# The first load of a batched matmul as one transfer of 128 partitions, or as one of 16 and one of 112

## The chip, the cores and the metric

The kernel runs on one core of a Trainium2 chip. The metric is the device time of one execution in microseconds (us), given as the median of several runs. A profile of one execution stands beside it; its span, from the first to the last instruction that it shows, is about 2 us shorter than the time. Inside the core, TensorE (PE) multiplies, VectorE (DVE) and ScalarE (ACT) copy and cast, GpSimd (POOL) prepares an identity matrix, and SyncE (SP) issues most transfers. All transfers of the core run on the same 16 DMA engines.

## The reference

Sixteen products of 512 x 512 matrices in float32; both operands come transposed.

```python
def setup_inputs():
    batch, m, k, n = 16, 512, 512, 512
    return {
        "a": np.random.randn(batch, k, m).astype(np.float32),
        "b": np.random.randn(batch, n, k).astype(np.float32),
    }

def reference(a, b):
    return np.matmul(a.transpose(0, 2, 1), b.transpose(0, 2, 1)).astype(np.float32)
```

The inputs are 16.8 MB each and the output is 16.8 MB: 50.33 MB pass between HBM and SBUF, each byte once.

## The kernel before

Each engine has a program of its own, and they are tied by semaphores. SyncE loads a and b. The batch is taken in 16 items i; two items make a pair q (or p, for b). A load of a is either one item (1 MB, 128 partitions with a row of 8 KB each) or, for the pairs in WIDE, a whole pair (2 MB). A load of b is always a pair (2 MB). There are three buffers for each.

```python
    a_v = a.rearrange("b (ki ko) m -> b ki ko m", ko=KO)      # one item: 128 partitions x 8 KB
    a_w = a.rearrange("(p g) (ki r) m -> p (g ki) r m", g=2, r=2 * KO)
    WIDE = range(1, 6)
    LOADS = 3                                                 # buffers of a; PAIRS = 3 of b
    # ...
        def load_a(sp, i):
            q, g = divmod(i, 2)
            s, use = q % LOADS, q // LOADS
            if use:
                sp.wait_ge(summed, MO * (2 * (q - LOADS) + 1) + 1)
            if q in WIDE:
                sp.dma_start(a_sb[s][:], a_w[q]).then_inc(a_in[2 * s], 16)
            else:
                sp.dma_start(a_sb[s][:, g * KO:(g + 1) * KO], a_v[i]).then_inc(a_in[2 * s + g], 16)

        def loaded_a(q, g):                # semaphore and value that the cast of (q, g) waits for
            g = 0 if q in WIDE else g
            uses = [u for u in range(q + 1) if u % LOADS == q % LOADS and (g == 0 or u not in WIDE)]
            return a_in[2 * (q % LOADS) + g], 16 * len(uses)
```

SyncE issues the first item of a, then the first two pairs of b with the second item of a between or after them, and goes on in that manner; from the fourth pair on it waits for buffers to come free. At the end it issues the last stores.

```python
        def run_sp(sp):
            for i in range(B):
                if i == 0:
                    load_a(sp, 0)
                for p in ([0] if i == 0 else [(i + 1) // 2] if i % 2 and i + 1 < B else []):
                    if p >= PAIRS:
                        sp.wait_ge(turned, p - PAIRS + 1)
                    sp.dma_start(b_sb[p % PAIRS][:], b_v[p]).then_inc(b_in[p % PAIRS], 16)
                # ... wait for an earlier store
                if i and not (i % 2 and i // 2 in WIDE):
                    load_a(sp, i)
            # ... the stores of the last pairs; the last one waits for its copies:
            sp.wait_ge(last_go, 3)
            store(sp, H - 1, slice(1, 2))
```

ScalarE waits for a load of a and casts it to bfloat16; VectorE waits for a load of b and casts it. TensorE transposes b (128 x 128 at a time, against the identity), VectorE copies the result to SBUF, and TensorE multiplies. VectorE and ScalarE copy the sums out of PSUM, and the stores are issued by ScalarE and, for the last pairs, by SyncE.

```python
        def cast_a(act, i):
            q, g = divmod(i, 2)
            sem_, value = loaded_a(q, g)
            act.wait_ge(sem_, value)
            # ... act.copy(a_bf[i % 2] <- a_sb[q % LOADS])
```

Of the kernel before, what the change touches and what calls it, by code (L numbers as in the profile page):

```python
# [11 lines left out]
def kernel(  # L12
# [7 lines left out]
    P = 128  # L20
    B, K, M = a.shape
    _, N, _ = b.shape
    KO = K // P
# [12 lines left out]
    a_v = a.rearrange("b (ki ko) m -> b ki ko m", ko=KO)  # L36
# [4 lines left out]
    WIDE = range(1, 6)  # L41
    LOADS = 3
# [11 lines left out]
    with tc.tile_critical(sync_engine=nc.gpsimd.engine):  # L54
# [3 lines left out]
        a_sb = [sb(f"a_sb{s}", [P, 2 * KO, M], f32) for s in range(LOADS)]  # L58
# [12 lines left out]
        a_in = [sem(f"a_in{s}") for s in range(2 * LOADS)]  # L71
# [22 lines left out]
# [4 lines that stand above are left out]
            if use:  # L98

                sp.wait_ge(summed, MO * (2 * (q - LOADS) + 1) + 1)  # L100
            if q in WIDE:
                sp.dma_start(a_sb[s][:], a_w[q]).then_inc(a_in[2 * s], 16)
            else:
                sp.dma_start(a_sb[s][:, g * KO:(g + 1) * KO], a_v[i]).then_inc(a_in[2 * s + g], 16)

        def loaded_a(q, g):

            g = 0 if q in WIDE else g
            uses = [u for u in range(q + 1) if u % LOADS == q % LOADS and (g == 0 or u not in WIDE)]
            return a_in[2 * (q % LOADS) + g], 16 * len(uses)  # L110

        def run_sp(sp):
            for i in range(B):
# [8 lines that stand above are left out]
                if i % 2 == 0 and i // 2 >= OUTS:  # L122

                    sp.wait_ge(o_out[i // 2 % OUTS], 16 * (i // 2 // OUTS))
                if i and not (i % 2 and i // 2 in WIDE):
                    load_a(sp, i)

            for j in range(H - TAIL, H - 1):
                sp.wait_ge(summed, MO * (2 * j + 2) + 3)
                store(sp, j)  # L130

            sp.wait_ge(summed, MO * (B - 1) + 1)
            sp.wait_ge(half_go, 1)
            store(sp, H - 1, slice(0, 1))
            sp.wait_ge(last_go, 3)
            store(sp, H - 1, slice(1, 2))
# [17 lines left out]
# [5 lines that stand above are left out]
            x, to = a_sb[q % LOADS], a_bf[i % 2]  # L159
            act.wait_ge(sem_, value)  # L160
            if q in WIDE:
                own = slice(g * P // 2, (g + 1) * P // 2)
                for s in range(2):
                    copy = act.copy(to[s * P // 2:(s + 1) * P // 2], x[own, s * KO:(s + 1) * KO, :])  # L164
            else:
                copy = act.copy(to[:], x[:, g * KO:(g + 1) * KO, :])  # L166
            copy.then_inc(ac_go, 1)
# [150 lines left out]
```

## Time and profile before

| | |
|---|---|
| time, median of 3 runs | 124.49 us (124.38 to 124.84) |
| span of the profiled execution | 122.5 us |
| TensorE busy (matmuls and transposes) | 83.3 us, 68% |
| ScalarE busy | 66.9 us, 55% |
| VectorE busy | 56.0 us, 46% |
| bytes moved | 50.33 MB, 411 GB/s over the span |

The page divides the span into 40 slices of about 3 us. One row gives the mean busy share of the 16 DMA engines in each slice, in tenths (9 is 90% or more), the next what they moved in GB/s. A table of windows gives the same for any stretches of time: each line has the stretch, its length, the busy time and number of instructions of PE, PE's weight loads, DVE, ACT and POOL, then the clock that was granted to TensorE (1 is full speed), the DMA share and GB/s. A line of the timeline has the start, the duration, the engine (SPq is SyncE's issue of a transfer), the source line, the operation, and its target and source.

The transfers by kind, as the page lists them, with the median from issue to landing in the last column:

```profile
b_sb<-in_b_dram SPq DMA_DIRECT2D x8, 2048.0 KB, 20.4
a_sb<-in_a_dram SPq DMA_DIRECT2D x5, 2048.0 KB, 19.0
out_dram<-o_sb ACTq DMA_DIRECT2D x5, 2048.0 KB, 16.2
a_sb<-in_a_dram SPq DMA_DIRECT2D x6, 1024.0 KB, 16.2
```

Most of these durations are time in the queue behind earlier transfers. The very first load of a, which has nothing ahead of it, is the exception: it is issued at 0.89 us, and the cast that waits for it starts at 5.74 us.

### The profile page before, as it was taken

The numbers are of one execution on the slowest core, as the hardware profiler recorded it, in microseconds if no ns is written. First come the engines' busy times: TensorE is split into PE (matmuls) and PEld (weight loads), VectorE is DVE, ScalarE is ACT, GpSimd is POOL, SyncE is SP. The second block draws the span as 40 slices with busy tenths as digits, with TensorE's granted clock in tenths as the row PEclk, the third lists the DMA queues.
The fourth block names the chain that finished last, engine by engine and source line by source line (L and its number), as shares of the span: only waits on it lengthen the run. The fifth ranks groups of instructions, "written<-read, shape, count | busy, mean of one in ns | idle before, by whom it ended". The sixth has DMA issues, their size and how long they took to land. (4 is left out here: it accounts for less than half of the span.)

```text
span 122.5 us, 1093 instructions
## 1 busy us (share of the span) xinstructions
PE 83.3 (68%) x400; PEld 48.0 (39%) x400; DVE 56.0 (46%) x48; ACT 66.9 (55%) x44; POOL 0.7 (1%) x6
## 2 busy tenths in 40 slices
PE   0000949799799979979994950593999599798000
PEld 0000913464365446437543610131744464374000
DVE  0005272837839575692759340039295542703000
ACT  4140015684997999799797008997221864803000
POOL 2000000000000000000000000000000000000000
PEclk9999999999999999999999997569999999999855
DMA  3999999999999999999999999999999999999992
GB/s 67 447 428 428 415 442 428 434 428 428 428 428 428 428 428 415 407 423 431 442 407 452 420 431 436 431 409 452 423 409 428 428 428 425 428 428 428 428 425 120
DMA packets 4928, 50.33 MB, mean 411 GB/s; under 512 B 448, under 2 KB 448, under 8 KB 448
## 3 DMA queue, kind: packets, MB, share of 16 engines
q1 hardware_dynamic: 3568, 39.85, 77.1%
q10 hardware_dynamic: 1360, 10.49, 20.2%
HBM read 33.55 MB, written 16.78 MB: 411 GB/s over the span
## 5 line engine op out<-in xcount | busy, mean ns | idle before, releaser
L256 PE MATMUL o_ps<-bt_sb,a_bf 128*128 128x512 bf16 x256 | 64.9, 402 | 8.7 <-PEq L231 8.2
L256 PEld LDWEIGHTS o_ps<-bt_sb,a_bf 128*128 128x128 bf16 x256 | 28.8, 116 | 38.7 <-issue 16.4
L164 ACT CAST a_bf<-a_sb 64x2048 bf16<-64x2048 f32 x20 | 38.0, 1899 | 7.6 <-DMA a_sb<-in_a_dram 7.3
L242 PE MATMUL bt_ps<-identity,b_bf 128*128 128x128 f32 x144 | 22.1, 302 | 20.8 <-PEq L231 20.8
L176 DVE COPY o_sb<-o_ps 128x1024 f32<-128x1024 f32 x16 | 19.6, 1224 | 29.9 <-PE o_ps L256 29.9
L242 PEld LDWEIGHTS bt_ps<-identity,b_bf 128*128 128x128 f32 x144 | 20.5, 209 | 25.7 <-issue 24.5
L189 DVE CAST b_bf<-b_sb 128x2048 bf16<-128x2048 f32 x16 | 19.4, 1219 | 22.7 <-DMA b_sb<-in_b_dram 22.7
L176 ACT COPY o_sb<-o_ps 128x1024 f32<-128x1024 f32 (+1 forms) x17 | 16.4, 964 | 19.7 <-PE o_ps L256 19.6
L166 ACT CAST a_bf<-a_sb 128x2048 bf16<-128x2048 f32 x6 | 11.4, 1901 | 18.4 <-DMA a_sb<-in_a_dram 18.4
L198 DVE COPY bt_sb<-bt_ps 128x1024 f32<-128x1024 f32 x16 | 19.4, 1214 | 2.7 <-PE bt_ps L242 2.7
L166 ACT ACT_TABLE_LOAD x1 | 1.3, 1283 | 0.9 <-PEq L302 0.9
L143 POOL TENSOR_SCALAR_AFFINE_SELECT identity<-identity 128x128 f32<-128x128 f32 x1 | 0.3, 292 | 0.2 <-POOL identity L141 0.2
L141 POOL MEMSET identity<- 128x128 f32 x1 | 0.2, 204 | 0.7 <-POOLq L54 0.7
L302 POOL MEMSET const-bfloat16-1.0<- 128x1 bf16 x1 | 0.1, 102 | 0.0
L302 POOL MEMSET const-uint8-127<- 128x1 uint8 x1 | 0.1, 102 | 0.0
L302 POOL MEMSET const-float32-0.0<- 128x1 f32 x1 | 0.1, 99 | 0.2 <-issue 0.2
L302 POOL MEMSET const-float32-1.0<- 128x1 f32 x1 | 0.1, 99 | 0.0
## 6 DMA issues: line engine op xcount, KB each, us to landing
b_sb<-in_b_dram SPq DMA_DIRECT2D x8, 2048.0 KB, 20.4
a_sb<-in_a_dram SPq DMA_DIRECT2D x5, 2048.0 KB, 19.0
out_dram<-o_sb ACTq DMA_DIRECT2D x5, 2048.0 KB, 16.2
a_sb<-in_a_dram SPq DMA_DIRECT2D x6, 1024.0 KB, 16.2
out_dram<-o_sb SPq DMA_DIRECT2D x2, 2048.0 KB, 13.3
out_dram<-o_sb SPq DMA_DIRECT2D x2, 1024.0 KB, 8.9
```

The costliest lines, as they stand in the source:

```text
L141: pool.memset(identity[:], 0.0).then_inc(id_go, 1)
L143: pool.affine_select(out=identity[:], in_=identity[:], compare_op=mybir.AluOpType.not_equal, fill=1.0, base=0, pattern=[[-1, P]], channel_ ...
L164: copy = act.copy(to[s * P // 2:(s + 1) * P // 2], x[own, s * KO:(s + 1) * KO, :])
L166: copy = act.copy(to[:], x[:, g * KO:(g + 1) * KO, :])
L176: copy(o_sb[i // 2 % OUTS][:, i % 2, rm, :], o_ps[h][:, p, :]).then_inc(go, 1)
L189: dve.tensor_copy(to, x).then_inc(bc_go, n)
L198: dve.tensor_copy(bt_sb[g][:].rearrange("p j (ni r) -> p j ni r", r=NR), bt_ps[:].rearrange("p j r (g ni) -> p g j ni r", g=2)[:, g],).the ...
L242: last = pe.transpose(bt_ps[:, j, r, :], w[:, r, j, :], identity[:])
L256: last = pe.matmul(o_ps[h][:, q, :], a_r[:, rk, 2 * h + q, :], bt_h[:, rk // 2, rk % 2, :], start=(rk == 0), stop=(rk == KO - 1),)
L302: nc = _bacc.Bacc("TRN2", target_bir_lowering=False, num_devices=1)
```

## The change

The first load of a, one transfer of 128 partitions, becomes two: partitions 0 to 15, which gives each of the 16 DMA engines one descriptor (one row of 8 KB), and then partitions 16 to 127. It is meant to let the DMA engines begin sooner[...]. Both count on the same semaphore, so that every wait for this buffer half has 16 more to wait for. No other load is altered.

```diff
             if use:
 
                 sp.wait_ge(summed, MO * (2 * (q - LOADS) + 1) + 1)
-            if q in WIDE:
+            if i == 0:
+
+                for part in (slice(0, 16), slice(16, P)):
+                    sp.dma_start(a_sb[s][part, :KO], a_v[0, part]).then_inc(a_in[0], 16)
+            elif q in WIDE:
                 sp.dma_start(a_sb[s][:], a_w[q]).then_inc(a_in[2 * s], 16)
             else:
                 sp.dma_start(a_sb[s][:, g * KO:(g + 1) * KO], a_v[i]).then_inc(a_in[2 * s + g], 16)
@@ -107,7 +111,7 @@
 
             g = 0 if q in WIDE else g
             uses = [u for u in range(q + 1) if u % LOADS == q % LOADS and (g == 0 or u not in WIDE)]
-            return a_in[2 * (q % LOADS) + g], 16 * len(uses)
+            return a_in[2 * (q % LOADS) + g], 16 * (len(uses) + (q % LOADS + g == 0))
```

## The prediction

> **What bounds the kernel now.** I read the page in this order: the row of DMA shares in part 2, the chain that ended last, then the DMA issues in order of time, and last a table of windows over the first microseconds and the end. Part 2 settles the bound, the windows settle what this change can reach.
>
> ```profile
> DMA  3999999999999999999999999999999999999992
> GB/s 67 447 428 428 415 442 428 434 428 428 428 428 428 428 428 415 407 423 431 442 407 452 420 431 436 431 409 452 423 409 428 428 428 425 428 428 428 428 425 120
> HBM read 33.55 MB, written 16.78 MB: 411 GB/s over the span
> ```
>
> Every slice but the first and the last is full. The sixteen DMA engines never run dry, although TensorE is busy only 68% of the span and ScalarE 55%. The kernel is a stream of 50.33 MB at one constant rate, with a head before the stream and a tail behind it. The chain of waits agrees: it covers only about 6 us of a 122.5 us span and ends on the last ScalarE copy at 113.44 us. What comes after is the backlog of stores draining.
>
> The head, finely:
>
> ```profile
> 0.89 0.38 SPq L104 DMA_DIRECT2D a_sb<-in_a_dram  x1
> 1.32 0.89 SPq L121 DMA_DIRECT2D b_sb<-in_b_dram  x2
> 2.26 0.61 SPq L104 DMA_DIRECT2D a_sb<-in_a_dram  x1
> ```
>
> ```profile
> 1.80:1.90 0.10, 0.00 (x0) 0.00 (x0) 0.00 (x0) 0.10 (x1) 0.06 (x1) 1.00 0.00 0
> 1.90:2.00 0.10, 0.00 (x0) 0.00 (x0) 0.00 (x0) 0.10 (x1) 0.00 (x0) 1.00 5.76 655
> 2.00:2.10 0.10, 0.00 (x0) 0.00 (x0) 0.00 (x0) 0.10 (x1) 0.00 (x0) 1.00 0.00 0
> ...
> 2.40:2.50 0.10, 0.00 (x0) 0.00 (x0) 0.00 (x0) 0.00 (x0) 0.00 (x0) 1.00 0.64 246
> 2.50:2.60 0.10, 0.00 (x0) 0.00 (x0) 0.00 (x0) 0.00 (x0) 0.00 (x0) 1.00 1.20 328
> 2.60:2.70 0.10, 0.00 (x0) 0.00 (x0) 0.00 (x0) 0.00 (x0) 0.00 (x0) 1.00 0.28 82
> ...
> 3.30:3.40 0.10, 0.00 (x0) 0.00 (x0) 0.00 (x0) 0.00 (x0) 0.00 (x0) 1.00 1.54 655
> ```
>
> The last two columns are DMA share and GB/s. A packet is put whole into the window in which it starts, so both columns can be turned into packets. Between 1.90 and 2.00 us, 655 GB/s x 0.1 us = 65.5 KB: 8 packets of 8 KB (one row of a for one partition). Their time is 5.76 x 16 engines x 0.1 us = 9.2 us, so 1.15 us each. Then nothing starts for 0.4 us. Between 2.40 and 2.70 us, 246 + 328 + 82 = 656 GB/s over 0.1 us is again 8 packets; 2.12 x 1.6 = 3.39 us, so 0.42 us each. In the steady stream (3.30 to 3.40 us) 8 packets take 1.54 x 1.6 = 2.46 us, 0.31 us each. So eight engines start at about 1.95 us and hold their first packet until about 3.10; the other eight start at about 2.55 us and are done at about 2.97. On the average of the sixteen the first packet is done at 3.03 us, and from there the stream runs at 0.31 us a packet. That is the stretch which the change is aimed at.
>
> The tail:
>
> ```profile
> 2.90:120.20 117.30, 83.32 (x400) 47.97 (x400) 56.01 (x48) 65.57 (x43) 0.00 (x0) 0.95 1.01 427
> 120.20:121.00 0.80, 0.00 (x0) 0.00 (x0) 0.00 (x0) 0.00 (x0) 0.00 (x0) 0.50 0.15 62
> 121.00:122.50 1.50, 0.00 (x0) 0.00 (x0) 0.00 (x0) 0.00 (x0) 0.00 (x0) 0.50 0.00 0
> ```
>
> The stream ends at about 120.5 us while the last store was issued at 113.48 us, some 7 us earlier. The engines thus have 7 us of slack at the end, and a head shorter by x should make the end come x earlier, as long as no wait in between lets the queue run empty.
>
> [...] the issue ends at 0.89 + 0.38 = 1.27 us and the first packet starts at 1.90, 0.63 us later. [...]
>
> **The change part by part.** Removed: one issue of 128 rows, 1 MB. Added: an issue of 16 rows, 131 KB, and one of 112 rows, 0.92 MB, both on the same semaphore, and the first cast now waits for 32 instead of 16. Bytes and rows are the same; sixteen semaphore packets of 4 bytes are added (448 now, 464 then), one for each engine and at the end of a transfer, which I put at nothing. No engine instruction is added but one issue on SyncE.
>
> 1. The extra issue moves all later ones of SyncE by 0.43 us (0.89 to 1.32 us is the pitch now). Later loads are queued microseconds ahead of the engines: the first 2 MB of b are issued at 1.32 us but wait behind a, 1.05 MB or 2.5 us of stream. So this costs nothing for b and for what follows. The only part that can be late is the 112 rows.
> 2. The gain at most: all sixteen engines start their one row at 1.90 us and run on at 0.31 us each. The first row is then done at 2.21 us against 3.03: 0.82 us, 0.66% of 124.49.
> 3. What takes from it: each engine has work for only 0.31 us until rows of the second transfer arrive. That is issued at about 1.32 us. [...] If its packets are not held up as the first eight are now, the low half starts its second row at 2.35 to 2.4 us against 3.10 now (gain 0.7), the high half at 2.9 against 2.97 (gain 0.07). The mean is about 0.4 us.
> 4. If the second transfer's first packets are held up as those of the first transfer now are, all of the present head is repeated 0.43 us later, with 0.31 us of work done ahead of it: a loss of 0.12 us.
> 5. Compute does not move the end. The first cast of a has landed data at 5.74 us, but TensorE starts at 12 us, behind the first 2 MB of b, and that follows the stream.
>
> **The rivals.** (A) [...] a gain of about 0.4 us (step 3). For it: [...] the second group, which starts late but then runs its first packet at close to full rate. I give it 45%. (B) The head is a fixed latency of the first data from a cold start: the first eight packets are held for 1.15 us and all sixteen end between 2.8 and 3.2 us, as if something became available at about 2.5 to 2.8 us whatever had started. Then sixteen rows would be held as eight are now, the 112 rows would meanwhile queue up behind them, and the time stays within 0.1 us. I give it 30%. (C) Each transfer pays its own start-up (step 4): 0.1 us slower. I give it 25%; the separate issue of 0.43 us, longer than the 0.31 us of work in the small piece, speaks for it. (D) The end does not follow the head: the shift is lost in the drain, where engines finish between 120.2 and 121.0 us and the slowest sets the span. This halves A's effect rather than adding a new time. No rival with an engine as the new bound is credible, because no engine's work changes and the queue has 7 us of slack.
>
> **Range and chances.** Weights by sizes: 0.45 x 0.4 + 0.30 x 0 - 0.25 x 0.12 = 0.15 us, so 124.49 - 0.15 = 124.34, and with the runs' own skew upward (median 124.49, lowest 124.38) I say 124.3 us. The range takes the full gain of step 3 with some run noise below it, 123.85, and rival C with noise above it, 124.75; three runs before spread over 0.46 us. Two per cent is 2.5 us, three times the largest gain that the head can give (0.82 us), and no loss of that size is in sight: 1% for faster, 98% for the same, 1% for slower.
>
> **What would show it.** In the windows from 1.8 to 3.4 us of the changed kernel: under A sixteen packets (1310 GB/s over 0.1 us) start together near 1.9 us, take 0.3 to 0.5 us each, and a second wave follows at 2.3 us. Under B the sixteen start together but take about 1.1 us. Under C the small ones are quick, and a gap opens until 2.8 us or later before the next wave settles. The middle must stay at 427 GB/s and full in every slice, and the stream's end near 120.5 us must move by what the head gained; if the head moves and the end does not, step D has it. The prediction is wrong if the middle shows a slice below full, if rows of the 112-partition piece take well over 0.31 us each (an uneven spread over the engines), or if the time leaves the range at all, since the head has no more than 0.82 us to give.

## The result and the profile after

The changed kernel takes 125.52 us (median of 4 runs, 125.41 to 125.62) against 124.66 us (124.38 to 124.90) before: a ratio of 1.0069, 95% interval 1.0042 to 1.0097. It is 0.86 us slower, and outside the predicted range.

The page of the changed kernel, the rows of DMA share and rate and the total:

```profile
DMA  5989999999999999999999999999999999999992
GB/s 88 337 382 440 430 424 430 435 430 424 424 424 424 424 424 432 411 430 432 454 390 456 422 440 419 427 422 462 393 424 435 424 427 432 427 427 427 427 424 90
HBM read 33.55 MB, written 16.78 MB: 407 GB/s over the span
```

The rates differ from before in the second and third slices: 337 and 382 GB/s, where the kernel before has 447 and 428. A slice is 3.09 us, so about 110 and 46 GB/s less are 0.34 MB and 0.14 MB; the first slice has 21 GB/s, 0.06 MB, more. The net 0.42 MB is 1.0 us of the stream at 427 GB/s. From the fourth slice on the two kernels are alike. The row of DMA shares hardly shows this: it has 9 and 8 in those slices, because an engine that waits inside a packet counts as busy (a share of 3.64 for the window of 2.40 to 2.60 us below, whose packets take 1.06 us each). The bound has to be read from the GB/s.

Windows of the changed kernel (DMA share and GB/s are the last two columns):

```profile
1.90:2.10 0.20, 0.00 (x0) 0.00 (x0) 0.00 (x0) 0.20 (x1) 0.00 (x0) 1.00 2.71 655
2.10:2.40 0.30, 0.00 (x0) 0.00 (x0) 0.00 (x0) 0.08 (x1) 0.00 (x0) 1.00 0.00 0
2.40:2.60 0.20, 0.00 (x0) 0.00 (x0) 0.00 (x0) 0.00 (x0) 0.00 (x0) 1.00 3.64 451
2.60:3.50 0.90, 0.00 (x0) 0.00 (x0) 0.00 (x0) 0.00 (x0) 0.00 (x0) 1.00 0.39 73
...
6.50:121.00 114.50, 83.81 (x392) 48.09 (x400) 56.02 (x48) 65.58 (x43) 0.00 (x0) 0.96 1.01 428
121.00:122.10 1.10, 0.00 (x0) 0.00 (x0) 0.00 (x0) 0.00 (x0) 0.00 (x0) 0.50 0.06 22
```

and two finer ones:

```profile
4.60:4.70 0.10, 0.00 (x0) 0.00 (x0) 0.00 (x0) 0.00 (x0) 0.00 (x0) 1.00 1.61 492
4.70:4.80 0.10, 0.00 (x0) 0.00 (x0) 0.00 (x0) 0.00 (x0) 0.00 (x0) 1.00 1.56 492
```

Counted as in the prediction: the sixteen rows of the short transfer all start between 1.90 and 2.10 us (655 GB/s x 0.2 us = 131 KB) and take 2.71 x 3.2 / 16 = 0.54 us each, so that each of the sixteen engines has one. The engines go straight on: 11 packets of the second transfer start at 2.40 to 2.60 us. But these are held for 3.64 x 3.2 / 11 = 1.06 us each, and in the 0.9 us after them only 8 packets start. Then, with all engines at work, a row of 8 KB takes 1.61 x 1.6 / 6 = 0.43 us and 1.56 x 1.6 / 6 = 0.42 us, where the kernel before has 0.31. So there are two losses: a second start-up, and slow rows for as long as the 112-partition piece lasts. Two windows of each kernel, first before and then after, give their sizes:

```profile
1.50:4.00 2.50, 0.00 (x0) 0.00 (x0) 0.00 (x0) 0.68 (x1) 0.29 (x1) 1.00 0.77 242
4.00:8.00 4.00, 0.00 (x0) 0.00 (x0) 0.00 (x0) 1.90 (x1) 0.00 (x0) 1.00 1.04 438
```

```profile
1.50:4.00 2.50, 0.00 (x0) 0.00 (x0) 0.00 (x0) 0.68 (x1) 0.30 (x1) 1.00 0.84 193
4.00:8.00 4.00, 0.00 (x0) 0.00 (x0) 0.00 (x0) 1.05 (x1) 0.00 (x0) 1.00 1.05 371
```

By 4.0 us, when the start-up is over, the changed kernel is behind by (242 - 193) x 2.5 us = 0.12 MB, which is 0.3 us of the stream at 427 GB/s. From 4 to 8 us, where the rest of the 112 rows runs, it falls behind by (438 - 371) x 4 us = 0.27 MB, another 0.6 us.

The cast that waits for this load starts at 6.95 us (5.74 before), and the stream thins out at 121.0 us, as it did at 120.2 before.

### The profile page after: what moved, and what is told of

Its sections match the earlier page's. It is cut to its first block, busy times and chain, and to the rows that moved or that the text cites. A ratio compares the mean times of both kernels' runs of the same rounds, so it can differ in the third digit from the quotient of the medians.

```text
span 123.5 us, 1086 instructions
## 1 busy us (share of the span) xinstructions
PE 83.8 (68%) x392; PEld 48.1 (39%) x400; DVE 56.0 (45%) x48; ACT 66.9 (54%) x44; POOL 0.7 (1%) x6
## 5 line engine op out<-in xcount | busy, mean ns | idle before, releaser
L260 PE MATMUL o_ps<-bt_sb,a_bf 128*128 128x512 bf16 x248 | 64.1, 407 | 9.5 <-PEq L235 8.5
L180 ACT COPY o_sb<-o_ps 128x1024 f32<-128x1024 f32 (+1 forms) x17 | 16.4, 965 | 19.7 <-PE o_ps L260 19.6
```

The costliest lines, as they stand in the source:

```text
L180: copy(o_sb[i // 2 % OUTS][:, i % 2, rm, :], o_ps[h][:, p, :]).then_inc(go, 1)
L260: last = pe.matmul(o_ps[h][:, q, :], a_r[:, rk, 2 * h + q, :], bt_h[:, rk // 2, rk % 2, :], start=(rk == 0), stop=(rk == KO - 1),)
```

## The experiments

Two theories stood at the outset. **Start-up:** each transfer that finds an empty queue pays for its beginning, and the 16 rows are too little work to hide the second. **Partitions:** the rows of a piece that is not all 128 partitions are slow wherever it stands, and how slow goes by which partitions it has. How slow each set would be (partitions 0 to 15 four times as slow as a whole transfer, a half or every eighth partition twice) was my estimate ahead of its run; the runs below measure it. In the expectations, the figures ahead of those for Start-up, or for causes that go by numbers, are those of Partitions. Times are given against the kernel before, run on the same chip.

**1. Four late splits.** The first load is whole; items 12 to 15 go as 16 and 112 partitions.

```diff
+    PIECES = {i: (slice(0, 16), slice(16, 128)) for i in (12, 13, 14, 15)}
-            if q in WIDE:
+            if i in PIECES:
+                for part in PIECES[i]:
+                    sp.dma_start(a_sb[s][part, g * KO:(g + 1) * KO], a_v[i, part]).then_inc(a_in[2 * s + g], 16)
+            elif q in WIDE:
...
-            return a_in[2 * (q % LOADS) + g], 16 * len(uses)
+            return a_in[2 * (q % LOADS) + g], 16 * sum(len(PIECES.get(2 * u + g, [0])) for u in uses)
```

> The first load is whole again; four loads late in the stream (items 12 to 15) go as 16 and 112 partitions. [...] rows of 8 KB take 0.40 to 0.43 us instead of 0.31 wherever the split stands, and each of the four costs 0.4 to 0.9 us: 1.6 to 3.5 us slower than before. Start-up: each new transfer pays for its beginning only when the queue is empty; late in the stream that is hidden, so within 0.2 us of before.

Measured: 128.84 us against 124.34, ratio 1.0363 (1.0324 to 1.0402): 4.5 us, 1.1 us for each split. Its windows where the split loads run, and after them:

```profile
80.00:90.00 10.00, 6.51 (x23) 3.61 (x22) 4.77 (x5) 4.64 (x3) 0.00 (x0) 0.68 1.02 397
90.00:100.00 10.00, 7.81 (x40) 4.51 (x38) 7.02 (x6) 2.26 (x2) 0.00 (x0) 0.97 1.03 367
100.00:110.00 10.00, 8.99 (x37) 4.38 (x38) 3.09 (x3) 6.24 (x5) 0.00 (x0) 0.83 0.99 348
110.00:124.40 14.40, 6.84 (x37) 4.11 (x35) 2.85 (x3) 2.22 (x4) 0.00 (x0) 0.89 1.01 426
```

The engines are occupied throughout (share about 1.0), yet move 348 to 397 GB/s instead of 427, and return to 426 when the splits are over; what they fall short in these three windows is 1.7 MB, 4.0 us of the 4.5. Start-up alone falls: none of the split transfers starts into an empty queue here.

**2. The same split at the second load.** As in 1, with `PIECES = {1: (slice(0, 16), slice(16, 128))}`.

> The first load is whole; the second load of a (item 1), issued while the engines have several transfers queued, goes as 16 and 112 partitions. [...] about 1.1 us slower than before, as each of the four late splits was (4.5 us over four); that would be more than the 0.86 us at the first load, where the quick start of the 16 rows gives part of it back. Start-up: hidden in the queue, so within 0.15 us of before.

Measured: 126.40 us against 124.38, ratio 1.0165 (1.0144 to 1.0186): 2.0 us. Start-up falls again. Partitions holds, but the expectation was short by half: the same split costs over twice as much at the second load as at the first. It also costs nearly twice as much as each late split (1.1 us); why these were cheaper was not tested.

**3. Two halves of the first load.** `PIECES = {0: (slice(0, 64), slice(64, 128))}`.

> The first load goes as 64 and 64 partitions. [...] rows take up to 0.62 us and the time is 1 to 2.5 us over before, more than with the change. Start-up: each engine has four rows, 1.24 us of work, while the second transfer is prepared, which hides most of it: at most 0.2 us slower, and rather faster than before[...].

Measured: 126.54 us against 124.34, ratio 1.0179 (1.0160 to 1.0197): 2.2 us slower. A window of it while the halves run:

```profile
4.00:6.00 2.00, 0.00 (x0) 0.00 (x0) 0.00 (x0) 0.00 (x0) 0.00 (x0) 1.00 1.01 221
```

The sixteen engines are at work throughout (share 1.01), and move 221 GB/s: about half of 427.

**4. Two halves of the first pair of b.** The same with twice the bytes.

```diff
-                    sp.dma_start(b_sb[p % PAIRS][:], b_v[p]).then_inc(b_in[p % PAIRS], 16)
+                    for part in ((slice(0, 64), slice(64, 128)) if p == 0 else (slice(0, 128),)):
+                        sp.dma_start(b_sb[p % PAIRS][part], b_v[p][part]).then_inc(b_in[p % PAIRS], 16)
```

(with 16 more to wait for on this buffer's semaphore)

> The first load of a is whole; the first pair of b, 2 MB, goes as 64 and 64 partitions. [...] twice the bytes of the earlier run with two halves of a, so twice its 2.2 us: 4 to 5 us slower than before, with rows of 16 KB taking about 1.2 us instead of 0.61. Start-up or the number of transfers: within 0.2 us of before, since it is issued behind the first load of a.

Measured: 129.48 us against 124.38, ratio 1.0407 (1.0388 to 1.0427): 5.1 us. The pair's 2.1 MB at half the rate take 4.9 us more (from 8 to 14 us the windows have 202 GB/s). The loss goes with the bytes (2.2 us for the 1 MB of experiment 3), not with the number of transfers.

**5. Partitions 0 to 15 by themselves.** Four extra transfers of these sixteen partitions, issued into the running stream (the waits on their semaphore count them too).

```diff
+                for n in range(4 if i == 1 else 0):
+                    sp.dma_start(o_sb[3 + n // 2][slice(0, 16), n % 2], a_v[0, slice(0, 16)]).then_inc(a_in[1], 16)
```

> The first load is whole. Behind the first pair of b, where the engines have several microseconds of work queued, four extra transfers of partitions 0 to 15 are issued (128 KB each of a read once more, into buffers not yet in use). Their bytes alone cost 4 x 0.31 = 1.24 us. [...] 4 x 1.24 = 4.9 us. Start-up: hidden in the queue, so 1.2 to 1.4 us.

Measured: 129.22 us against 124.39, ratio 1.0392 (1.0369 to 1.0416): 4.83 us.

**6. Every eighth partition.** As in 5, with `slice(0, P, 8)` in place of `slice(0, 16)`.

> The same four extra transfers of 16 rows, but on every eighth partition (0, 8, ... 120)[...]. [...] 4 x 0.62 = 2.5 us slower than before, half of what partitions 0 to 15 cost. Any cause that goes by the number of partitions, descriptors or transfers: the same as with partitions 0 to 15.

Measured: 126.88 us against 124.39, ratio 1.0196 (1.0174 to 1.0218): 2.49 us. The windows of both while the extra rows run; first partitions 0 to 15:

```profile
11.00:12.00 1.00, 0.00 (x0) 0.00 (x0) 0.39 (x1) 0.00 (x0) 0.00 (x0) 1.00 1.01 107
12.00:13.00 1.00, 0.02 (x1) 0.05 (x1) 1.00 (x2) 0.00 (x0) 0.00 (x0) 1.00 1.01 107
```

then every eighth partition:

```profile
11.00:12.00 1.00, 0.00 (x0) 0.00 (x0) 0.89 (x1) 0.00 (x0) 0.00 (x0) 1.00 1.07 221
```

Same number of partitions, rows, bytes and transfers, and nearly the same DMA share (1.01 and 1.07); 107 against 221 GB/s, a quarter and about half of the 427 in the stream. This settles Partitions against every cause that goes by counts of partitions, rows or transfers. The two also read different rows of a in HBM (sixteen neighbours, or every eighth). That was not varied by itself, but it does not explain experiment 4, whose halves read 1 MB in one stretch, as a whole load of a does, and still ran at half rate. Why one set of sixteen partitions is slower than another was not shown.

**7. The 112 partitions by themselves.** One extra transfer of partitions 16 to 127 into the running stream.

```diff
+                if i == 1:
+                    sp.dma_start(o_sb[4][16:, 0], a_v[0, 16:]).then_inc(a_in[1], 16)
```

> The first load is whole. Behind the first pair of b one extra transfer of partitions 16 to 127 is issued (0.92 MB of a read once more, into a buffer not yet in use). Its bytes alone cost 7 x 0.31 = 2.16 us. [...] 3.1 to 3.4 us[...]. With the cost of the 16 rows (1.24 us each time[...]) this has to add up to the 2.0 us that the split cost at the second load. Start-up: 2.2 us.

Measured: 127.55 us against 124.39, ratio 1.0252 (1.0227 to 1.0277): 3.16 us. A window while the extra rows run:

```profile
11.00:12.00 1.00, 0.00 (x0) 0.00 (x0) 1.00 (x1) 0.00 (x0) 0.00 (x0) 1.00 0.94 262
```

262 KB are 32 rows, of 0.94 x 16 / 32 = 0.47 us each. The sum closes: the 112 rows cost 3.16 - 2.15 = 1.0 us beyond their bytes (0.92 MB at 427 GB/s), the 16 rows 4.83 / 4 - 0.31 = 0.9 us. Together 1.9 us, and the split at the second load measured 2.0.

**8. The 16 rows ahead of a whole first load.** This keeps the quick start and the second start-up, and takes away the 112-partition piece.

```diff
                 if i == 0:
+                    sp.dma_start(o_sb[4][:16, 0], a_v[0, :16]).then_inc(a_in[0], 16)
                     load_a(sp, 0)
```

> A transfer of 16 rows is put ahead (128 KB of a read a second time, into a buffer that is not yet in use), and then the whole first load of 128 partitions. The extra bytes cost 0.31 us at the stream's rate. [...] 0.3 to 0.7 us slower than before, and rows of the first load near 0.31 us. Start-up of a second transfer: the whole cost of the change stays and the extra bytes come on top, 1.0 us slower or more.

Measured: 124.85 us against 124.38, ratio 1.0044 (1.0025 to 1.0064): 0.47 us slower, of which 0.31 is bytes. Its first microseconds:

```profile
1.90:2.10 0.20, 0.00 (x0) 0.00 (x0) 0.00 (x0) 0.20 (x1) 0.00 (x0) 1.00 1.65 655
2.10:2.30 0.20, 0.00 (x0) 0.00 (x0) 0.00 (x0) 0.07 (x1) 0.00 (x0) 1.00 0.02 0
2.30:2.50 0.20, 0.00 (x0) 0.00 (x0) 0.00 (x0) 0.00 (x0) 0.00 (x0) 1.00 2.87 328
2.50:3.00 0.50, 0.00 (x0) 0.00 (x0) 0.00 (x0) 0.00 (x0) 0.00 (x0) 1.00 0.00 0
3.00:3.30 0.30, 0.00 (x0) 0.00 (x0) 0.00 (x0) 0.00 (x0) 0.00 (x0) 1.00 0.64 218
3.30:5.50 2.20, 0.00 (x0) 0.00 (x0) 0.00 (x0) 0.00 (x0) 0.00 (x0) 1.00 0.97 410
```

The sixteen rows start together and take 1.65 x 3.2 / 16 = 0.33 us: a quick start, as wished. Behind them the head of the kernel before is repeated whole: eight packets at about 2.4 us held for 2.87 x 3.2 / 8 = 1.15 us, a gap, eight more at about 3.15 us that take 0.64 x 4.8 / 8 = 0.38 us. The second start-up costs 0.47 - 0.31 = 0.16 us (by the interval of the ratio, 0 to 0.5 us), and the slow rate that partitions 0 to 15 have in the stream (107 GB/s in experiment 5) costs nothing visible here.

**9. The two pieces in the other order.** `PIECES = {0: (slice(0, 112), slice(112, 128))}`.

> The first load goes as 112 partitions first and then 16. [...] 0.4 to 0.9 us slower than before, with rows of about 0.4 us. Start-up: the first transfer has the head that the kernel before has, and that of the 16 is hidden behind seven rows for each engine, so within 0.15 us of before.

Measured: 125.69 us against 124.34, ratio 1.0104 (1.0087 to 1.0121): 1.35 us, more than either expectation. It speaks for Partitions and against Start-up. The size is in keeping with 7 and 5 if partitions 112 to 127 are as slow as 0 to 15, which was not measured by itself: the 16 rows now stand inside the stream, where those of experiment 5 cost 0.9 us beyond their bytes, and not in the head. The window in which the last of the 112 rows and the 16 rows run agrees:

```profile
5.00:6.50 1.50, 0.00 (x0) 0.00 (x0) 0.00 (x0) 0.00 (x0) 0.00 (x0) 1.00 1.05 180
```

It is short of 427 GB/s by 0.37 MB, 0.9 us.

**10. A cut by columns.** Both pieces have all 128 partitions: 2 KB and then 6 KB of each row.

```diff
+                for part in (slice(0, 1), slice(1, 4)):
+                    sp.dma_start(a_sb[s][:, g * KO:(g + 1) * KO][:, part], a_v[i][:, part]).then_inc(a_in[2 * s + g], 16)
```

> The first load goes in two transfers again, but cut by columns: all 128 partitions with 2 KB each, then all 128 with 6 KB. [...] the rows of the second run at full rate, and the time is within 0.3 us of before. Start-up: a second transfer behind a short first one is held anew, 0.3 us or more slower, most of the 0.86 us that the change cost if that is the whole cause.

Measured: inconclusive. The five runs lie in two groups, 124.59 and 124.65 us, and 126.22 to 126.54 us, against 124.34 us; the ratio is 1.0111 (1.0050 to 1.0171). The profile is of the run of 124.65 us, 0.3 us over before, so it cannot say what the other group lost. The first group would fit Partitions and the second Start-up. No run beat the kernel before.

**11. Two halves from two queues.** SyncE issues partitions 0 to 63, ScalarE 64 to 127, at the same time.

```diff
+            act.dma_start(a_sb[0][64:, :KO], a_v[0, 64:]).then_inc(a_in[0], 16)
             cast_a(act, 0)
```

> The first load of a goes as 64 partitions from SyncE and the other 64 from ScalarE, issued at the same moment on two queues. If the engines take packets from the two queues in turn, rows of both halves are under way together [...]: then the start is earlier[...] and the time is up to 0.4 us below before. If the two halves still run one after the other [...], it is 1 to 2.2 us slower, as with two halves from one queue.

Measured: 126.46 us against 124.38, ratio 1.0170 (1.0149 to 1.0191): 2.1 us slower, like the two halves from one queue. The halves did not mix. The packets by queue (q1 is SyncE's, q10 ScalarE's), first from 2.0 to 4.3 us, then from 4.3 to 6.7 us:

```profile
q1 hardware_dynamic: 64, 0.52, 95.4%
```

```profile
q10 hardware_dynamic: 64, 0.52, 101.6%
q1 hardware_dynamic: 16, 0.00, 0.8%
```

All 64 rows of SyncE's half ran before the first of ScalarE's, although both were issued within 0.01 us. What decides the order is open: in the next experiment 24 and 16 packets of the two queues had started by 4.0 us.

**12. Two whole transfers at once.** Nothing is split; ScalarE issues the first load of a while SyncE issues the first pair of b.

```diff
                 if i == 0:
-                    load_a(sp, 0)
...
+            load_a(act, 0)
             cast_a(act, 0)
```

> No load is split; the first load of a is issued by ScalarE at the moment at which SyncE issues the first pair of b, so that both begin about 0.9 us into the span. If each queue's start-up runs by itself, the engines have two packets to work on while each is prepared and b is ready 0.43 us sooner: 0.1 to 0.5 us faster than before. If one unit prepares both in turn, within 0.1 us of before, or slower by the hold of two transfers instead of one.

Measured: 124.51 us against 124.39, ratio 1.0007 (0.9997 to 1.0016): the same. Both issues stand at 0.89 and 0.90 us. The first microseconds in steps, and then in sum:

```profile
1.50:2.00 0.50, 0.00 (x0) 0.00 (x0) 0.00 (x0) 0.50 (x1) 0.29 (x1) 1.00 0.75 197
2.00:2.50 0.50, 0.00 (x0) 0.00 (x0) 0.00 (x0) 0.50 (x1) 0.00 (x0) 1.00 1.16 328
2.50:3.00 0.50, 0.00 (x0) 0.00 (x0) 0.00 (x0) 0.13 (x1) 0.00 (x0) 1.00 0.24 49
...
1.50:4.00 2.50, 0.00 (x0) 0.00 (x0) 0.00 (x0) 1.13 (x1) 0.29 (x1) 1.00 0.73 210
```

The first rows are those of b, of 16 KB: 6 and 10 packets by 2.5 us, so all sixteen engines hold one, of which each takes 0.93 us (1.16 x 8 / 10, in the second line) where the stream has 0.61 (16.4 KB at 427 / 16 = 26.7 GB/s). So more bytes are started early, but by 4.0 us they are fewer than before (210 and 242 GB/s). The head is not shortened by a second queue. None of the twelve runs gave a version that beats the kernel before.

## Why the prediction was wrong

**What held.** The bound did: one saturated stream, whose end follows its beginning. The middle ran at 428 GB/s, the head and the first load lost about 1 us, and the end came about 0.8 us later; no engine became a bound and rival D did not occur. Step 1 held as well: the added issue moved all later ones by 0.47 us (the first pair of b at 1.79 us), and nothing waited for them. The quick start was right in part: sixteen engines started together just after 1.90 us, as rival A had it.

**The first part that failed: step 3.** It took the two distances of the trace before, 1.01 us from the issue to the first eight packets and 1.61 us to the other eight, counted them from 1.32 us (2.33 and 2.9 us), and let the second transfer run freely from there. In its place came step 4, rival C, which I gave only 25%: experiment 8 shows the whole head repeated about half a microsecond later, with 0.31 us of work done ahead of it. I put 0.12 us on that. It measured 0.16 us there, with an interval of 0 to 0.5 us, and the profile of the change is 0.3 us behind by 4.0 us. So the mechanism was there and its size of the right order, but it explains only a fifth to a third of the 0.86 us.

**The step that carried the error.** Steps 2 to 4 take 0.31 us for every row of both pieces, and the change's list of costs has "bytes and rows are the same". What the partitions of a piece do to its rate was missing from the sum. I assumed the same count of rows for each DMA engine, one and then seven, and took that for an even load. For pieces of 16 and 64 partitions experiments 3 to 6 show that what limits is where the rows land: 107 GB/s for partitions 0 to 15, 221 for every eighth partition, 221 and 202 for halves. The 0.31 us a row had been measured for whole transfers of 128 partitions alone. The 112 rows took 0.42 us instead, and the piece costs 1.0 us beyond its bytes inside the stream.

That their slowness has the same cause as that of the 16 rows and the halves is my estimate and was not shown: no run varied the partitions of such a piece by themselves.

I had looked for what the head could gain or lose, and for nothing in the stream behind it. The runs show a loss there, 2.2 us with two halves. My list of what would make the prediction wrong did name rows of well over 0.31 us, but for an uneven spread over engines, and gave it no weight in the range.

**Why 0.86 and not 2.0 us.** At the second load the split costs 2.0 us, of which the sixteen rows are 0.9 us beyond their bytes (experiment 5). At the head these rows show nothing of it: they took 0.54 us each, and 0.33 us in experiment 8, where experiment 5 has 1.01 x 16 / 13 = 1.24 us. In experiment 8 their 131 KB went through in about 0.5 us, some 260 GB/s, more than twice what the same partitions gave in the stream. Either what slows them in the stream does not act on these first bytes, or the records of the packets end before it does, and the wait for the second transfer hides it; no run separates the two. What remains is 1.0 + 0.16 = 1.16 us by the experiments and 0.6 + 0.3 = 0.9 us by the profile, against 0.86 us measured, whose interval reaches from 0.5 to 1.2 us.

**What stays open.** What holds the first packets of a transfer for 1.1 us at an empty queue is not settled. Two groups of eight engines that start one after the other, on which rival A rested, fit the kernel before and experiment 8 (at 1.9 and 2.5 us, and at about 2.4 and 3.15 us), but in experiment 12 all sixteen engines had a packet by 2.5 us and were held all the same. Nor is the hold always 1.1 us: in experiment 3 the first sixteen rows took 0.56 us each, though they started only after 2.2 us, and in experiment 10 the first rows, of 2 KB, took 0.11 us. The two levels of the cut by columns are unexplained.

## What to carry to other kernels

In a stream that is bound by transfers, a load cut by partitions was not free here even with all sixteen DMA engines at work: at shares of 0.94 to 1.01, partitions 0 to 15 moved at 107 GB/s, a half at 221 and the 112 at 262, where whole transfers had 427. Measure the rate of the sets of partitions that a cut makes, or keep all 128 in a piece. That alone brought no gain here: the cut by columns does so and was not faster (124.59 to 126.54 us against 124.34). A short first transfer started quickly (sixteen rows of 0.54 us, from 1.90 us on) but did not cover the start-up of the next one: it had 0.31 us of work by the stream's rate, and the next one's first packets, from 2.40 us on, were held for 1.06 us each. Read the rate and not the busy share: the engines show as full at 107 GB/s as at 427.

## What the runs showed of the hardware

The rate of a transfer went by its partitions: partitions 0 to 15 gave 107 GB/s, every eighth partition 221, two halves of 64 partitions 221, and whole transfers 427 GB/s. The two halves, one from each of two queues, cost 2.1 us, as much as from one queue (2.2 us). And the same split into 16 and 112 rows cost 2.0 us at the second load and 1.1 us each for four late ones, but 0.86 us at the start of the stream: there the 16 rows took 0.54 us each, and not 1.24 us as in the stream.
